# Feed-forward by seven products: adding transfers, splits and loads of the weight sums moved in the order of steps, and one set of token splits moved beside the down products

## The chip, the cores and the metric

The kernel runs on one core of one Trainium2 chip. The metric is the device time of one execution in microseconds (us), here the median of three runs. TensorE (PE) multiplies, VectorE (DVE), ScalarE (ACT) and GpSimd (POOL) do the rest, and SyncE (SP) and POOL issue transfers from memory (HBM) to the on-chip buffers.

## The reference

One inference step of a two-layer trunk (width 1024) over 128 context tokens and 512 latent tokens, 640 in all, with the same weights. Each layer has a first feed-forward, a mixer (a gated DeltaNet, an attention and a recurrent unit side by side), and a second feed-forward. The change touches the feed-forwards alone:

```python
def swiglu(h, w_gu, w_down):
    g, u = jnp.split(h @ w_gu, 2, axis=-1)
    return (jax.nn.silu(g) * u) @ w_down
x = x + 0.5 * mod[:, 2] * swiglu(h, lp['ffn1_wgu'], lp['ffn1_wd'])
```

with `w_gu` of 1024 x 5632 and `w_down` of 2816 x 1024, in f32. The vectors `mod` come from a conditioning vector times `w_mod` (1024 x 9216) for each layer.

## The kernel before, in words

**Split numbers.** An f32 product is made of three faster ones: each operand is split into a high part (ACT rounds a copy, `wh`) and a low part (DVE takes the difference, `wl`), and `three` adds high*high, high*low and low*high. A 128 x 512 piece of weights is thus read by one ACT and one DVE instruction, the split, before PE can use it.

**Seven products.** The 640 tokens are two halves of 320, named p and q, and a column of 128 outputs has a gate part G and an up part U, each with two halves of the 1024 inputs (G1, G2, U1, U2). The four block products of a column are replaced by seven products of sums of tokens with sums of weights (P1, P2, Q3, Q4, Q5, Q6, Q7). Each is 12 matmuls of 320 columns. The sums of tokens are made once for a feed-forward (`sums7`, `split7`). The sums of weights are made by transfers: a tile X is loaded with U2, then U1 is added by a transfer that POOL issues (`more`), and this is the weight of Q5; then G1 is added (the weight of Q6) and then G2 (the weight of Q3). A tile Y is loaded with U1 and gets G1 added (the weight of Q7). P1, P2 and Q4 use G1, G2 and U2 as loaded. A column so takes five loads by SP, four adding transfers by POOL and seven splits. An adding transfer has to wait until the split before it has read the tile.

**Steps.** `ffn7` writes the order of the work by hand. The first columns (chunk 0, 3 or 6 of 22, and 2 more where `then` is 2) go through eight plain products (`eight`), with their down products behind chunk 0. All other columns go by sevens, in chunks of 3 or 4, and each chunk is followed by the 16 down products of 12 matmuls that use it (the last by its own). One product is one step. In the middle of a chunk a column has this order, with its own P1 as step 0: P1, Q4 of the column before, Q5, Q6, P2, Q7, Q3; the next column's P1 is step 7. A column begun before a run of down products has P1 to P2 ahead of it and the rest behind.

`put(t, fn)` hangs other work on a step, and after the matmuls of step t its list is issued, for each engine in this order (`s.pin`, `keep_in_program_order`). Work on steps below 0 and the tail is not pinned: there a scheduler with its own cost model orders the engines, and within a tag buffers are handed out in the order of the program. Among the hung-on work are copies of finished sums out of PSUM by ACT, which the next product into the same bank waits for: t1 after P1 (step 1, before Q6 adds to the bank at step 3), V after Q6 (step 4, before Q7 at step 5). The columns of `mod` for later layers hang on steps too: one transfer of 512 KB and two DVE instructions over 128 x 1024 each (`mod_cols`).

**Buffers.** `w`, raw pieces of weights: 3. `wh` and `wl`: 7 each (`WB`). X: class "B", 4, which the token sums hold until `split7` has read them. Y: two halves of one tile (`rw`).

**Lines.** 157 is `act`, 160 `add`, 164 `more`, 167 `dma`, 170 `tt`, 178 `stt`, 187 `mm`. In the profile t_B is X (and the token sums), t_A on POOL is Y, w a raw piece, tg a copy out of PSUM, th a working tile, t_H the split tokens, t_W and t_C the columns of `mod`; wacc and acc are PSUM banks, wacc that of P1, Q6, Q7 and Q4.

Of the kernel before, what the change touches and what calls it, by code (L numbers as in the profile page):

```python
# [60 lines left out]
K2 = KT // 2  # L61
# [38 lines left out]
class Trunk:  # L100
# [408 lines left out]
    def ffn7(s, wgu, wd, i, spec, done):  # L509
        p, q = HO  # L510
# [8 lines left out]
        def sums():  # L519
            r = [s.A(4 * H, True).v(2, 2, r=True) for _ in range(3 * K2 // 2)]  # L520
            s.s7 = [[r[(3 * k + j) // 2][:, (3 * k + j) % 2] for j in range(3)] for k in range(K2)]

        def rest():
            for k in range(K2):
                v = s.h[k].v(2, r=True)
                s.split(v[:, 0, s.hs(q)], v[:, 1, s.hs(q)], s.xq[k][:, 0])

        acts, w = {}, {0: s.ahead}

        def eight(m0, n, beside):  # L530
            for mi, h in s.halves(n, 2, 0):
                f = m0 + mi
                if f not in w:
                    w[f] = [s.prep(wgu[f, e], KT) for e in range(2)]
                    acts[f] = s.A(2 * T, True)
                g = s.proj(w[f][0], h)
                u = s.proj(w[f][1], h, ps=s.bank())
                s.gated(acts[f], h, g[:, :H], u[:, :H])
                beside()

        acts[0] = s.A(2 * T, True)
        todo = [s.later[:K2], s.later[K2:]] + [[lambda k=k: s.sums7(k)] for k in range(K2)]
        if not then:
            sums()
            todo += [[lambda k=k: s.split7(k)] for k in range(K2)]
        s.first = True

        def beside():
# [18 lines left out]
        if then:  # L567
            sums()
            todo += [[lambda k=k: s.split7(k)] for k in range(K2)]
            eight(n0, then, lambda: [fn() for fn in todo.pop(0)])  # L570
        rest()


        order = []
# [2 lines left out]
        for ci, ch in enumerate(chunks):  # L577
# [19 lines left out]
            else:  # L597
# [3 lines left out]
                a, b = os[:2], os[2:]  # L601
# [6 lines left out]
        def put(t, fn, *a, late=0):  # L608
            at.setdefault(t, ([], [], []))[late].append((fn, a))
# [11 lines left out]
        def tile(f, n, src):  # L621

            def fn():
                ws[f, n] = s.hilo()
                m = len(chunks[f]) if type(n) is int else WK
                wh, wl = ws[f, n]
                s.split(wh[:, :m], wl[:, :m], src()[:, :m])
            return fn

        for f in range(plain, NM):  # L630
            P1, Q5, P2, Q6, Q3, Q7, Q4 = [pos[f, n] for n in ("P1", "Q5", "P2", "Q6", "Q3", "Q7", "Q4")]
            a = P1 - 5
            r, d = {}, {}

            def wsrc(n, f=f):
                return wgu[f, "GU".index(n[0])][:, K2 * (n[1] == "2"):K2 * (n[1] == "2") + K2, :]

            def load(n, src, f=f, r=r, wsrc=wsrc):
                r[n] = rw[:, f % 2] if n == "Y" else s.slots.alloc(WK * P, False, "B").v(WK) if n == "X" else s.raw()
                s.dma(r[n], wsrc(src))  # L640

            def more(n, src, r=r, wsrc=wsrc):
                s.more(r[n], wsrc(src))
            for t, fn, n, src in ((a - 8, load, "X", "U2"), (a - 6, more, "X", "U1"), (a - 3, load, "G1", "G1"),
                                  (a - 2, load, "Y", "U1"), (a + 1, more, "Y", "G1"), (a + 1, load, "G2", "G2"),
                                  (a + 2, more, "X", "G1"), (a + 6, more, "X", "G2"), (max(a + 7, Q4 - 8), load, "U2", "U2")):
                put(t, fn, n, src)


            def tg(n, f=f, d=d):  # L650
                d[n] = s.norm.tile([P, H], F32, name="tg", tag="tg", bufs=3)
                return d[n]

            def th(n, d=d):
                d[n] = s.norm.tile([P, H], F32, name="th", tag="tmp", bufs=4)
                return d[n]
            put(P1 + 1, lambda d=d, tg=tg, f=f: s.act(tg("t1"), prods[f, "b"]))
            put(Q5 + 1, lambda d=d, tg=tg, f=f: s.act(tg("t5"), prods[f, "c"]))
            put(Q6 + 1, lambda d=d, tg=tg, f=f: s.act(tg("V"), prods[f, "b"]))
            put(P2 + 1, lambda d=d, f=f: s.tt(prods[f, "a"], d["t1"], prods[f, "a"], ALU.add))  # L660
            put(Q3 + 1, lambda d=d, f=f: s.tt(prods[f, "c"], d["V"], prods[f, "c"], ALU.add))
            put(Q7 + 1, lambda d=d, f=f: s.tt(d["t5"], d["t5"], prods[f, "b"], ALU.add))

            put(P2 + 2, lambda d=d, th=th, f=f: s.act(th("p"), prods[f, "a"], AF.Tanh, scale=0.5))
            put(P2 + 3, lambda d=d, f=f: s.stt(d["p"], d["p"], 1.0, prods[f, "a"], ALU.add, ALU.mult))
            put(Q3 + 2, lambda d=d, th=th, f=f: s.act(th("q"), prods[f, "c"], AF.Tanh, scale=0.5))
            put(Q3 + 3, lambda d=d, f=f: s.stt(d["q"], d["q"], 1.0, prods[f, "c"], ALU.add, ALU.mult))
            put(Q3 + 3, lambda d=d: s.stt(d["q"], d["q"], -1.0, d["t5"], ALU.mult, ALU.mult))
            put(Q4 + 1, lambda d=d, f=f: s.stt(d["p"], d["p"], -1.0, prods[f, "b"], ALU.mult, ALU.mult))

            def out(f, h):
                if f not in acts:
                    acts[f] = s.A(2 * T, True)
                return acts[f].v(2, r=True)[:, :, s.hs(h)]
            put(Q3 + 4, lambda d=d, f=f: s.act(out(f, q)[:, 0], d["q"]))
            put(Q3 + 4, lambda d=d, f=f: s.tt(out(f, q)[:, 1], d["q"], out(f, q)[:, 0].bitcast(F32), ALU.subtract))
            put(Q4 + 2, lambda d=d, f=f: s.act(out(f, p)[:, 0], d["p"]))
            put(Q4 + 3, lambda d=d, f=f: s.tt(out(f, p)[:, 1], d["p"], out(f, p)[:, 0].bitcast(F32), ALU.subtract))

            for n, x, t in (("P1", "G1", a), ("Q5", "X", a + 1), ("P2", "G2", a + 4), ("Q6", "X", a + 5),  # L680
                            ("Q7", "Y", max(a + 6, Q7 - 5)), ("Q3", "X", max(a + 9, Q3 - 5)), ("Q4", "U2", max(a + 10, Q4 - 5))):
                put(t, tile(f, n, lambda r=r, x=x: r[x]), late=2)
        downs = {}
        for t, x in enumerate(order):
# [12 lines left out]
        n, end = len(s.todo), min(tails) - 8  # L697
        for e, (mc, j, f) in enumerate(s.todo):
            t = e * end // n
# [13 lines left out]
        for t, x in enumerate(order):  # L713
            s.pin = t < min(tails)
            if len(x) == 2:
                f, n = x
# [1047 lines left out]
```

## Time and profile before

| what | value |
|---|---|
| time, median of 3 runs | 3141.28 us (3139.18 to 3144.94) |
| profiled execution: time, span | 3145.61 us, 3143.8 us |
| PE busy, of the span | 3035.8 us, 97% |
| DVE, ACT, POOL busy | 2320.0, 1355.3, 310.2 us |
| granted TensorE clock, mean | 0.989 |

The stretches in which the columns go by sevens, with their down products, are from 208 to 515 us (first feed-forward of layer 0, 14 columns), 1210.5 to 1608 us (second of layer 0, 19 columns), 1778 to 2074 us (first of layer 1, 14 columns) and 2745 us to the end (second of layer 1, 19 columns). The rest of the span is chunk 0, the mixers and the start. A row of instructions gives the start, the duration, the engine, the line and the operation, and in brackets the idle time of the engine before it and what ended it.

### The profile page before, as it was taken

The numbers are of one execution on the slowest core, as the hardware profiler recorded it, in microseconds if no ns is written. First come the engines' busy times: TensorE is split into PE (matmuls) and PEld (weight loads), VectorE is DVE, ScalarE is ACT, GpSimd is POOL, SyncE is SP. The second block draws the span as 40 slices with busy tenths as digits, with TensorE's granted clock in tenths as the row PEclk, the third lists the DMA queues.
The fourth block names the chain that finished last, engine by engine and source line by source line (L and its number), as shares of the span: only waits on it lengthen the run. The fifth ranks groups of instructions, "written<-read, shape, count | busy, mean of one in ns | idle before, by whom it ended". The sixth has DMA issues, their size and how long they took to land. (4 is left out here: it accounts for less than half of the span.)

```text
span 3143.8 us, 54878 instructions
## 1 busy us (share of the span) xinstructions
PE 3035.8 (97%) x20654; PEld 2860.5 (91%) x20654; DVE 2320.0 (74%) x4804; ACT 1355.3 (43%) x2812; POOL 310.2 (10%) x350
## 2 busy tenths in 40 slices
PE   8999999999999999999989999999999999999999
PEld 5999998998887988999989999989989879899999
DVE  6769888767757877777887688786676587866665
ACT  5233335446544443333452333443465454544433
POOL 2011110000000021111120111100000000221111
PEclk9999999999999999999999999999999999999999
DMA  5458773454322416777715577634543224176654
GB/s 223 157 156 224 214 207 107 141 157 125 122 72 62 144 68 173 186 187 189 182 64 167 152 198 196 175 107 130 160 126 100 68 69 145 59 164 152 149 139 127
DMA packets 309000, 451.47 MB, mean 144 GB/s; under 512 B 102989, under 2 KB 147869, under 8 KB 307997
## 3 DMA queue, kind: packets, MB, share of 16 engines
q1 hardware_dynamic: 262076, 357.97, 35.8%
q0 software_dynamic: 38016, 69.22, 13.3%
q10 hardware_dynamic: 8640, 20.76, 1.8%
q8 instruction: 163, 2.67, 0.3%
q14 instruction: 105, 0.85, 0.1%
HBM read 411.87 MB, written 35.96 MB: 142 GB/s over the span
## 5 line engine op out<-in xcount | busy, mean ns | idle before, releaser
L187 PE MATMUL wacc<-t_H,wh 128*128 128x320 f32 x4512 | 1035.0, 314 | 41.7 <-ACT t_H L157 17.3
L187 PEld LDWEIGHTS wacc<-t_H,wh 128*128 128x128 f32 x4512 | 757.8, 188 | 77.2 <-ACT t_H L157 20.7
L187 PE MATMUL acc<-t_A,wh 128*128 128x320 f32 x3440 | 761.5, 308 | 0.3 <-ACT t_A L157 0.3
L187 PE MATMUL wacc<-t_H,wl 128*128 128x320 f32 (+1 forms) x2256 | 702.8, 312 | 3.0 <-DVE wl L170 3.0
L157 ACT ACTIVATE wh<-w 128x512 fp32r<-128x512 f32 (+2 forms) x730 | 439.4, 608 | 572.9 <-PE acc L187 221.3
L170 DVE TENSOR_TENSOR wl<-w,wh 128x512 fp32r<-128x512 f32 (+2 forms) x730 | 483.5, 667 | 170.6 <-ACT wh L157 168.2
L187 PEld LDWEIGHTS acc<-t_A,wh 128*128 128x128 f32 x3440 | 575.5, 188 | 1.1 <-ACT t_A L157 0.5
L187 PE MATMUL acc<-t_A,wl 128*128 128x320 f32 x1720 | 529.8, 308 | 0.2 <-DVE wl L170 0.2
L187 PE MATMUL wacc<-t_A,wh 128*128 128x320 f32 x1984 | 458.6, 313 | 24.9 <-ACT tg L157 19.4
L187 PEld LDWEIGHTS wacc<-t_H,wl 128*128 128x128 f32 (+1 forms) x2256 | 423.8, 188 | 9.8 <-DVE wl L170 4.2
L187 PE MATMUL acc<-t_H,wh 128*128 128x320 f32 x1760 | 400.6, 311 | 0.1
L187 PEld LDWEIGHTS wacc<-t_A,wh 128*128 128x128 f32 x1984 | 336.7, 189 | 35.4 <-ACT tg L157 23.1
L187 PEld LDWEIGHTS acc<-t_A,wl 128*128 128x128 f32 x1720 | 322.6, 188 | 0.4 <-DVE wl L170 0.4
L187 PE MATMUL wacc<-t_A,wl 128*128 128x320 f32 x992 | 309.2, 312 | 0.0
L164 POOL DMA_DIRECT2D t_B<-in_wgu x198 | 194.1, 985 | 1145.4 <-DVE wl L170 682.0
L178 DVE SCALAR_TENSOR_TENSOR t_A<-acc,mG,t_A 128x128 f32<-128x128 f32 (+1 forms) x480 | 201.6, 446 | 138.4 <-PE acc L187 130.6
L187 PEld LDWEIGHTS acc<-t_H,wh 128*128 128x128 f32 x1760 | 299.7, 190 | 1.5 <-ACT wh L157 0.8
L187 PE MATMUL acc<-t_H,wl 128*128 128x320 f32 x880 | 274.7, 313 | 11.2 <-DVE wl L170 11.0
L157 ACT ACTIVATE wh<-t_B 128x512 fp32r<-128x512 f32 x198 | 124.4, 628 | 304.8 <-DMA t_B<-in_wgu 253.0
L170 DVE TENSOR_TENSOR wl<-t_B,wh 128x512 fp32r<-128x512 f32 x198 | 136.2, 688 | 118.5 <-ACT wh L157 118.2
L187 PEld LDWEIGHTS wacc<-t_A,wl 128*128 128x128 f32 x992 | 187.9, 189 | 3.0 <-issue 1.4
L187 PEld LDWEIGHTS acc<-t_H,wl 128*128 128x128 f32 x880 | 166.9, 190 | 16.7 <-DVE wl L170 16.6
(203 smaller groups left out, 3514.7 us busy)
## 6 DMA issues: line engine op xcount, KB each, us to landing
w<-in_wgu SPq DMA_DIRECT2D x286, 256.0 KB, 4.0
t_W<-in_wmod SPq DMA_DIRECT2D x128, 512.0 KB, 4.5
t_B<-in_wgu POOLq DMA_DIRECT2D x198, 256.0 KB, 4.9
w<-in_win SPq DMA_DIRECT2D x168, 256.0 KB, 3.0
w<-in_wd SPq DMA_DIRECT2D x144, 256.0 KB, 3.2
t_B<-in_wgu SPq DMA_DIRECT2D x66, 256.0 KB, 3.9
t_A<-in_wgu SPq DMA_DIRECT2D x66, 256.0 KB, 5.3
t_A<-in_wgu POOLq DMA_DIRECT2D x66, 256.0 KB, 5.2
```

Of the source, the lines that this page charges most:

```text
L157: return s.order(s.nc.scalar.activation(out=out, in_=in_, func=func, **kw))
L164: return s.order(s.nc.gpsimd.dma_start(out=out, in_=in_, accum_op=ALU.add))
L170: return s.order(s.nc.vector.tensor_tensor(out=out, in0=a, in1=b, op=op))
L178: return s.order(s.nc.vector.scalar_tensor_tensor(out=out, in0=a, scalar=sc, in1=b, op0=op0, op1=op1, **kw))
L187: return s.order(s.nc.tensor.matmul(out, lhsT, rhs, start=start, stop=stop, **kw))
```

## The change

It changes the steps on which a column's transfers and splits hang, and the place of `rest`, the splits of the q tokens' sums (four ACT and four DVE instructions over 128 x 320). Steps count from the column's own P1; the value before stands first.

| what | before | after |
|---|---|---|
| load U2 to X; add U1 | -13; -11 | -15; -13 |
| add G1 to X; add G2 to X | -3; 1 | -6; -1 |
| load U1 to Y; add G1 to Y | -7; -4 | -9; -7 |
| load G1; G2; U2 as loaded | -8; -4; 2 | -8; -5; 0 |
| split for P1; Q5; P2; Q6 | -5; -4; -1; 0 | -4; -7; -1; -2 |
| split for Q7; Q3; Q4 | 1; 4; 5 | 1; 3; 4 |

Q7, Q3 and Q4 are split later where down products come between. `rest` is now four pieces, hung on four of the down products of chunk 0 where `then` is 0 (the second feed-forwards); where it is 2 they stay behind the plain products.

```diff
-        def rest():
-            for k in range(K2):
-                v = s.h[k].v(2, r=True)
-                s.split(v[:, 0, s.hs(q)], v[:, 1, s.hs(q)], s.xq[k][:, 0])
+        def rest(k):
+            v = s.h[k].v(2, r=True)
+            s.split(v[:, 0, s.hs(q)], v[:, 1, s.hs(q)], s.xq[k][:, 0])
...
-            todo += [[lambda k=k: s.split7(k)] for k in range(K2)]
+            todo += [[lambda k=k: s.split7(k)] for k in range(K2)] + [[lambda k=k: rest(k)] for k in range(K2)]
...
-        rest()
+            for k in range(K2):
+                rest(k)
...
-            a = P1 - 5
...
-            for t, fn, n, src in ((a - 8, load, "X", "U2"), (a - 6, more, "X", "U1"), (a - 3, load, "G1", "G1"),
-                                  (a - 2, load, "Y", "U1"), (a + 1, more, "Y", "G1"), (a + 1, load, "G2", "G2"),
-                                  (a + 2, more, "X", "G1"), (a + 6, more, "X", "G2"), (max(a + 7, Q4 - 8), load, "U2", "U2")):
+            for t, fn, n, src in ((P1 - 15, load, "X", "U2"), (P1 - 13, more, "X", "U1"), (P1 - 8, load, "G1", "G1"),
+                                  (P1 - 9, load, "Y", "U1"), (P1 - 7, more, "Y", "G1"), (P1 - 5, load, "G2", "G2"),
+                                  (P1 - 6, more, "X", "G1"), (P1 - 1, more, "X", "G2"), (max(P1, Q4 - 9), load, "U2", "U2")):
...
-            for n, x, t in (("P1", "G1", a), ("Q5", "X", a + 1), ("P2", "G2", a + 4), ("Q6", "X", a + 5),
-                            ("Q7", "Y", max(a + 6, Q7 - 5)), ("Q3", "X", max(a + 9, Q3 - 5)), ("Q4", "U2", max(a + 10, Q4 - 5))):
+            for n, x, t in (("Q5", "X", P1 - 7), ("P1", "G1", P1 - 4), ("Q6", "X", P1 - 2), ("P2", "G2", P1 - 1),
+                            ("Q7", "Y", max(P1 + 1, Q7 - 5)), ("Q3", "X", max(P1 + 3, Q3 - 5)), ("Q4", "U2", max(P1 + 4, Q4 - 5))):
```

## Rows read from the trace of the kernel before

**Rows 1.** The page, whole span: busy us, share, instructions of each engine.

```profile
PE 3035.8 (97%) x20654; PEld 2860.5 (91%) x20654; DVE 2320.0 (74%) x4804; ACT 1355.3 (43%) x2812; POOL 310.2 (10%) x350
```

**Rows 2.** Stretches: length, busy us (instructions) of PE, PEld, DVE, ACT, POOL, clock, DMA, GB/s.

```profile
208.00:515.00 307.00, 293.07 (x1948) 288.41 (x1948) 263.31 (x542) 119.55 (x247) 47.17 (x53) 0.99 0.75 202
1210.50:1608.00 397.50, 379.06 (x2514) 371.44 (x2512) 305.38 (x618) 156.12 (x325) 63.83 (x73) 0.99 0.68 177
1778.00:2074.00 296.00, 289.67 (x1951) 287.52 (x1950) 231.23 (x475) 119.81 (x248) 47.28 (x53) 0.99 0.71 182
2745.00:3143.80 398.80, 393.60 (x2678) 392.52 (x2677) 249.29 (x508) 155.54 (x323) 66.44 (x76) 1.00 0.60 146
```

**Rows 3.** Waits of PE, 208 to 515: total us, times, longest us.

```profile
PE wacc L187 <- ACT tg L157: 10.0, 10, 5.0
PE acc L187 <- DVE wl L170: 3.9, 5, 0.9
```

**Rows 4.** Waits of PE, 1210.5 to 1608.

```profile
PE wacc L187 <- ACT tg L157: 12.0, 14, 3.3
PE acc L187 <- DVE wl L170: 4.7, 9, 0.9
PE wacc L187 <- DVE wl L170: 1.7, 1, 1.7
```

**Rows 5.** Waits of PE, 1778 to 2074.

```profile
PE wacc L187 <- ACT tg L157: 3.4, 2, 3.3
PE acc L187 <- DVE wl L170: 1.2, 2, 0.9
```

**Rows 6.** Waits of PE, 2745 to the end.

```profile
PE wacc L187 <- ACT tg L157: 1.4, 2, 0.9
```

**Rows 7.** Stretches from the first Q6 to the first Q7, columns as in rows 2.

```profile
216.92:223.20 6.28, 6.28 (x24) 6.28 (x25) 2.13 (x4) 2.79 (x6) 2.52 (x3) 0.52 0.87 153
1220.34:1226.70 6.36, 6.36 (x24) 6.36 (x25) 2.33 (x4) 2.27 (x5) 3.57 (x4) 0.51 0.52 104
1785.50:1790.60 5.10, 5.10 (x24) 5.10 (x25) 2.13 (x4) 2.79 (x6) 2.53 (x3) 0.67 0.82 127
```

**Rows 8.** Timeline of PE at 1250: a Q6 in the run of columns.

```profile
1250.17 0.56 PE L187 MATMUL wacc<-t_A,wh 128*128 128x320 f32 x2 [1.10 <-ACT tg L157]
```

**Rows 9.** Timeline of ACT: splits for Q6 at 214 and 1249, then t1 and V.

```profile
214.29 0.63 ACT L157 ACTIVATE wh<-t_B 128x512 fp32r<-128x512 f32 x1 [7.10 <-DMA t_B<-in_wgu]
...
1248.84 0.63 ACT L157 ACTIVATE wh<-t_B 128x512 fp32r<-128x512 f32 x1 [5.43 <-DMA t_B<-in_wgu]
...
1249.69 0.43 ACT L157 ACTIVATE tg<-wacc 128x320 f32<-128x320 f32 x1
...
1253.93 0.43 ACT L157 ACTIVATE tg<-wacc 128x320 f32<-128x320 f32 x1
```

**Rows 10.** Timeline of POOL at 1240 and 1250: G1 and G2 added to X.

```profile
1240.15 0.86 POOL L164 DMA_DIRECT2D t_B<-in_wgu  x1 [1.92 <-DVE wl L170]
1250.48 0.86 POOL L164 DMA_DIRECT2D t_B<-in_wgu  x1 [9.47 <-DVE wl L170]
```

**Rows 11.** Waits of ACT, 1231 to 1608, the longest in total.

```profile
ACT wh L157 <- DMA t_B<-in_wgu: 78.9, 18, 8.2
```

**Rows 12.** Tile t_B, 1231 to 1608: its transfers.

```profile
DMA to landing us min/median/max: 3.6/4.9/9.2
```

**Rows 13.** Stretches of one column each, columns as in rows 2.

```profile
372.97:388.80 15.83, 13.12 (x87) 12.33 (x85) 12.65 (x25) 6.37 (x14) 3.51 (x4) 1.00 0.86 220
...
1258.54:1273.57 15.03, 13.12 (x86) 12.34 (x85) 10.46 (x21) 6.37 (x14) 2.62 (x3) 1.00 0.74 170
2841.00:2853.40 12.40, 12.40 (x87) 12.40 (x86) 7.91 (x18) 1.98 (x4) 1.83 (x3) 1.00 0.63 166
```

**Rows 14.** Stretch up to the first Q6 of layer 0's second feed-forward, columns as before.

```profile
1196.50:1217.00 20.50, 18.58 (x124) 17.82 (x122) 20.14 (x45) 2.31 (x4) 1.73 (x2) 1.00 0.52 170
```

**Rows 15.** Groups of DVE, 1189 to 1212: the low parts of the moved token splits.

```profile
L170 DVE TENSOR_TENSOR t_H<-t_A,t_H 128x320 fp32r<-128x320 f32 x4 | 1.8, 482 | 0.0
```

## The prediction

> **What bounds the kernel now.** I read the page first: PE is busy 97% of the span [rows 1], so a change pays only where PE stands still or runs at its lower clock. Then the stretches: by busy against length, PE is idle 13.9 us in the first feed-forward of layer 0 (call it A), 18.4 in the second (B), 6.3 in the first of layer 1 (C) and 5.2 in the last (D) [rows 2]. Then the waits of PE in each: nearly all idle time is one product waiting either for a copy out of PSUM by ACT ("tg", 10.0, 12.0, 3.4 and 1.4 us in A, B, C, D) or for the low part of a split by DVE ("wl", 3.9 in A, 4.7 and 1.7 in B, 1.2 in C) [rows 3 to 6]. That is 13.9 + 18.4 + 4.6 + 1.4 = 38.3 us.
>
> The longest of these waits, 5.0, 3.3 and 3.3, stand at the first Q6 of A, B and C, and behind each PE runs on a granted clock of 0.52, 0.51 and 0.67, its lower level of 1.2 GHz for all or part of it: two products of 24 matmuls take 6.28, 6.36 and 5.10 us [rows 7]. A column of seven products without a wait takes 12.40 us [rows 13], a step 12.40/7 = 1.77, two steps 3.54. The lower clock so costs 2.7 + 2.8 + 1.6 = 7.1 us. **All that could come back is 38.3 + 7.1 = 45.4 us:** 7.7 (5.0 + 2.7) at the start of A, 7.8 (3.3 + 1.7 + 2.8) of B, 4.9 (3.3 + 1.6) of C, and in the run of columns 8.9 in A, 13.4 in B, 1.3 in C, 1.4 in D.
>
> Why a copy is late is read from three timelines. POOL issues the transfer that adds G1 to X at 1240.15, after a wait for the low part of Q5's split [rows 10]. ACT stands from 5.43 us before 1248.84 at the split for Q6, waiting for it; t1, the copy that Q6 needs, is behind it at 1249.69 [rows 9], and Q6 starts at 1250.17, 1.10 late [rows 8]. So the transfer took 8.7 us to land, and ACT's order turns this into a wait of PE. In B the split waits so 18 times, 78.9 us in all, up to 8.2 [rows 11]; ACT's idle time costs only what reaches t1, or V, which a late ACT and DVE then bring late too, and the low part for Q3 behind them.
>
> **The adding of G1 and the split for Q6.** From the add's step to Q6 are 6 steps before (-3 to 3), 10.6 us, and 9 after (-6 to 3), 15.9. The example needs 8.7 for landing and 1.3 (1248.84 to 1250.17) from split to product, 10.0, and came too late because the add itself waited for DVE. The longest wait in the runs cannot be more than the 3.3 of B's start, and 5.3 us of new lead covers it. Adding G2 and the split for Q3 gain one step between them (3 to 4), 1.77 us, and the low part for Q3 is hung one step sooner; the longest "wl" waits are 0.9 [rows 3, 4]. So these waits should go where DVE and the transfers have time to spare.
>
> They have in B, C and D: DVE is busy 305 of 397.5, 231 of 296 and 249 of 398.8 [rows 2]. In A it is not so plain. A column beside which two columns of modulation are made takes DVE 12.65 us and the transfer engines 0.86 x 15.83 = 13.6 us, against PE's 12.40; with one pair DVE takes 10.46 [rows 13]. Between such columns stand others and the down products, with less for both (A as a whole: 263 of 307, and 0.75) [rows 2], so lag is made and paid back, but some of A's waits will stay. I take half of A's 8.9, 4.5; of B's 13.4, 10.5 (a few columns with two pairs, and the one behind the start); 0.9 of C's 1.3 and 1.2 of D's 1.4. **Sum in the runs: 17.1.** The ends: 25.0 if all goes, and a loss, by the mechanism of the second rival.
>
> The Trainium skill, DMA: Bandwidth & Descriptors, section Anatomy of one DMA, fits a transfer from GpSimd as 2.0 us plus its bytes by 436,000 per us; by that 256 KB would land in 2.6 us, three steps of lead would have been ample, and the runs would give back nothing: with the 9 of the starts alone, 3132. The trace disagrees: the landings are 3.6 us at least, 4.9 in the median and 9.2 at most [rows 12].
>
> **The starts.** There the chain begins when `split7` sets a buffer of class B free, which the change does not move, and POOL's adds come one behind another. So the landing itself comes little sooner. But in A the split for Q6 starts at 214.29 [rows 9] and Q6 at 216.92 [rows 7]: 2.6 us, of which the split is 0.63 and 2.0 is t1 standing in ACT's pinned order behind it and behind what DVE owes. After the change that split hangs at -2, below step 0, where t1 need not stand behind it. I take this 2.0 off in A and C. Against it stands a new wait: V now comes behind the split for Q3 and that for the next P1. G2's add is issued when Q6's split is done, about when Q6 starts; 3.6 to land at least [rows 12], 0.63 and 0.63 for the two splits, 0.43 for V [rows 9] make 5.3 against the 3.54 of Q6 and P2: 1.8 us late, or none where the lower clock stretches the two products to 6.3. So A: 5.0 - 2.0 + 1.8 = 4.8 for 7.7, a gain of 3; C: 3.3 - 2.0 + 1.8 = 3.1 for 4.9, a gain of 2.
>
> In B DVE is full before the first products, 20.14 of 20.50 us [rows 14], and the wait of 1.7 there is P1's for its low part [rows 4]. Three or four of the moved token splits stand in this stretch, 0.48 each [rows 15]; hung on earlier down products they leave it 1.4 shorter. Q5's split is now ahead of P1's, which brings the add of G1 forward by about as much. I put P1's wait at 0.3, Q6's at 1.7, V's at 1.8, 3.8 for 7.8: a gain of 4. D has no wait at its start and loses none. **Sum of the starts: 9.** The ends: all 20.4; or 5.4 lost, three times 1.8, if nothing is sooner and the clock stays up.
>
> **What else moves.** SP's five loads and POOL's four adds per column stay as many, so do seven splits on ACT and seven on DVE. SP's X, Y and U2 are 2 steps sooner, but SP waits only for buffers. A raw piece is held 4 steps for 3: 12 of 21 buffer-steps a column. The split pairs are held 9 + 4 + 5 + 5 + 4 + 3 + 4 = 34 steps in all for 28, of 49, and in the last down products of a chunk all 7 pairs are held at once: two down, Q7, Q3 and Q4 of one column, Q5 and P1 of the next. I count this at nothing, since the eighth comes only after a down product has given one back. If one were missing, a split would wait for a down product of 1.77 at most, at 14 ends of chunks: 25 us. The moved token splits cost nothing more than they did, beside down products that keep PE busy 18.58 of 20.50 [rows 14]; without that cover they would hold `x_update` by 0.48 each, 2 us in a feed-forward. The new wait of t1 for the split of the next column's Q5, hung at step 0, is for an add issued 6 steps (10.6 us) before, longer than the longest landing of 9.2 [rows 12].
>
> **Sum:** 17.1 + 9 = 26 us off the profiled execution's 3145.6, so 3119.5; the median of the runs is 4.3 below that execution, so **3115**.
>
> **Rivals.** (1) Layer 0 stays bound by DVE and transfers: its runs give nothing, the rest 9 + 2.1 = 11, so 3130. For it the column at 373, both over PE's 12.40; against it B, where DVE has 92 us to spare [rows 2, 13]. Chance 0.21. The skill's fit above would lead to nearly the same time, 3132.
>
> (2) Slower: the split for Q3 now stands ahead of V, and V must end before step 5. From the add of G2 (-1) there are 6 steps, 10.6 us, less 0.63 + 0.63 + 0.43: 8.9 for POOL's wait and the landing. Past that every Q7 waits. If DVE lags 3 us with Q6's low part, a landing of 5.9 suffices, and the median is 4.9 [rows 12]. At 1 us for each of the 66 columns, 66 - 26: 3181; it decides from 0.4 us a column. Against it: G2's add is the first after POOL has been idle, 9.47 us in the example [rows 10], and V at 1253.93 [rows 9] was itself delayed by what goes. Chance 0.07.
>
> (3) Everything comes back, the clock at the starts too: 45, so 3096. For it the lead of 5.3 us against the 1.10 of the example [rows 8]; against it the starts, whose landing hardly moves. Chance 0.12.
>
> (4) No change: earlier loads and adds only make each other slower, landings grow by what the lead grows, and the same buffers set the pace; 3141. For it the transfers' share of 0.86 [rows 13]; against it C and D, which run nearly without waits at 0.71 and 0.60 [rows 2]. Chance 0.07.
>
> **The numbers.** My forecast, 3105 to 3127, has 0.53. About 0.2% (6.3 us) is what a measurement of this kernel can tell from no change; the forecast, (1) and (3) are faster by more: 0.86. (4) is the same, 0.07, and (2) slower, 0.07. The range goes from most of (3) to past (1): 3099 to 3135, with some of (3) and all of (2) and (4) outside.
>
> **What would show it.** In B the waits of PE for "tg" fall from 12.0 to some 5 or less, with the rest at the start, and ACT's wait for X (78.9) falls to a third. In A DVE's share rises and "wl" or "tg" waits stay. At the starts the split for Q6 no longer stands ahead of t1, and the first Q7 waits for V. It is wrong if new waits for "tg" stand at Q7 in the run of C or D, if a split waits for PE at the ends of chunks, or if POOL's adds wait for DVE as long as now and the landing of X still ends ACT's longest waits.

## The result, and the profile after

Time after: **3106.56 us** (median of 4 runs, 3104.22 to 3112.2); before, on the same chip, 3142.14 (3139.18 to 3144.94). The ratio is 0.9893, 95% interval 0.9881 to 0.9906: 35.6 us, 1.1%, faster. The profiled execution took 3105.24 us for 3145.61. The forecast was 3115, 3099 to 3135. So sign and size came out; of its two large terms one was half of what was measured and the other four times too large, and the reason given for the first was not the whole mechanism.

The page's first part after, to set against [rows 1]: PE is busy 15 us less with the same 20654 matmuls, and DVE, ACT and POOL run the same instructions as before, ACT 14 us longer in all.

```profile
PE 3020.4 (97%) x20654; PEld 2860.3 (92%) x20654; DVE 2322.1 (75%) x4804; ACT 1369.3 (44%) x2812; POOL 310.1 (10%) x350
```

To see where, both traces are cut at the same matmuls (there the order on PE did not change, but for seven matmuls at D's start; in the mixers between them some changed places): the start of a feed-forward runs from shortly ahead of its first P1 (in B 100 matmuls) to its first Q7, the run from there to the end of the stage. Columns as in [rows 2]. First two runs of before (A, B), whose answers in the second fence are lines two and four:

```profile
223.27:511.06 287.79, 278.83 (x1875) 274.83 (x1874) 256.65 (x529) 113.69 (x235) 43.66 (x49) 1.00 0.76 206
1226.74:1604.10 377.36, 364.15 (x2442) 357.87 (x2440) 293.07 (x593) 150.86 (x314) 59.40 (x68) 1.00 0.69 181
```

After: start and run of A, start and run of B, start of C.

```profile
207.55:222.72 15.17, 9.95 (x53) 9.69 (x51) 5.19 (x9) 5.66 (x12) 2.62 (x3) 0.77 0.81 194
222.72:498.31 275.59, 274.98 (x1876) 274.72 (x1875) 256.35 (x528) 114.27 (x234) 43.68 (x49) 1.00 0.78 215
1180.09:1205.84 25.75, 23.66 (x152) 23.39 (x150) 21.36 (x44) 6.11 (x12) 5.26 (x6) 0.93 0.64 171
1205.84:1565.88 360.04, 358.90 (x2441) 357.73 (x2440) 293.81 (x593) 155.70 (x314) 59.40 (x68) 1.00 0.73 190
1737.66:1754.88 17.22, 12.47 (x67) 12.21 (x66) 6.69 (x13) 7.14 (x16) 3.53 (x5) 0.80 0.86 188
```

The runs gave back 12.2 (A), 17.3 (B), 2.6 (C) and 1.7 us (D), 33.8 in all; the starts 0.1 (A, 15.29 before) and 4.9 (B, 30.67), while C's lost 2.6 (14.61). That is 36.2 of the profiled 40.4; 4.2 came elsewhere, where nothing was edited. In the profiled executions of all kernels below, the time outside these stretches, from the first matmul to the last, lay between 1720.7 and 1733.4, so 4 us there mean nothing.

The waits of PE after, in A, in B (three lines), in C and in D, to set against [rows 3 to 6] (total, times, longest):

```profile
PE wacc L187 <- ACT tg L157: 5.8, 2, 5.2
...
PE wacc L187 <- DVE wl L170: 2.1, 1, 2.1
PE wacc L187 <- ACT tg L157: 0.9, 2, 0.6
PE acc L187 <- DVE wl L170: 0.2, 1, 0.2
...
PE wacc L187 <- ACT tg L157: 4.7, 1, 4.7
...
PE wacc L187 <- DVE t_A L178: 0.2, 1, 0.2
```

What is left are the three starts (5.2 at the first Q6 of A, 4.7 of C, 2.1 at the first P1 of B) and 1.9 us in 66 columns.

### The profile page after: what moved, and what is told of

Same layout as the page of the kernel before. It is cut to its first block, busy times and chain, and to the rows that moved or that the text cites. A ratio compares the mean times of both kernels' runs of the same rounds, so it can differ in the third digit from the quotient of the medians.

```text
span 3103.4 us, 54871 instructions
## 1 busy us (share of the span) xinstructions
PE 3020.4 (97%) x20654; PEld 2860.3 (92%) x20654; DVE 2322.1 (75%) x4804; ACT 1369.3 (44%) x2812; POOL 310.1 (10%) x350
## 5 line engine op out<-in xcount | busy, mean ns | idle before, releaser
L187 PEld LDWEIGHTS wacc<-t_A,wh 128*128 128x128 f32 x1984 | 338.2, 190 | 22.6 <-ACT tg L157 11.7
L164 POOL DMA_DIRECT2D t_B<-in_wgu x198 | 173.2, 946 | 1140.8 <-DVE wl L170 614.2
L157 ACT ACTIVATE tg<-wacc 128x320 f32<-128x320 f32 x236 | 102.0, 433 | 169.1 <-PE wacc L187 143.1
```

Source lines behind the costliest of these rows:

```text
L157: return s.order(s.nc.scalar.activation(out=out, in_=in_, func=func, **kw))
L164: return s.order(s.nc.gpsimd.dma_start(out=out, in_=in_, accum_op=ALU.add))
L187: return s.order(s.nc.tensor.matmul(out, lhsT, rhs, start=start, stop=stop, **kw))
```

## The experiments

Each is given with its ratio to the kernel before, run on the same chip, and with what the same matmuls took, in us. The diffs show only the entries that change.

| kernel | ratio, 95% interval | A start, run | B start, run | C start, run | D run |
|---|---|---|---|---|---|
| before | 1 | 15.3, 287.8 | 30.7, 377.4 | 14.6, 286.9 | 382.6 |
| after | 0.9893 (0.9881 to 0.9906) | 15.2, 275.6 | 25.7, 360.0 | 17.2, 284.3 | 380.9 |
| E1 rest alone | 1.0001 (0.9989 to 1.0012) | 15.1, 288.0 | 27.5, 377.6 | 15.4, 290.5 | 381.0 |
| E2 steps alone | 0.9898 (0.9882 to 0.9915) | 14.9, 275.7 | 28.1, 359.0 | 17.9, 284.3 | 382.8 |
| E3 add of G1 three steps sooner | 0.9893 (0.9876 to 0.9910) | 15.2, 275.6 | 28.0, 363.2 | 17.1, 284.9 | 380.5 |
| E4 all but X | 1.0020 (1.0010 to 1.0030) | 16.5, 286.1 | 33.6, 371.8 | 17.5, 290.8 | 381.5 |
| E5 one step sooner | 0.9968 (0.9956 to 0.9979) | 13.8, 286.7 | 30.9, 369.7 | 15.5, 286.9 | 380.5 |
| E6 first in POOL's queue | 1.0009 (1.0000 to 1.0018) | 15.1, 291.6 | 29.1, 377.1 | 14.7, 290.5 | 380.9 |
| E7 and Q5's split sooner | 0.9901 (0.9884 to 0.9917) | 15.8, 276.9 | 25.2, 362.1 | 15.7, 284.9 | 380.5 |
| E8 t1 ahead of the splits | 0.9895 (0.9881 to 0.9909) | 10.7, 279.8 | 25.7, 361.0 | 14.1, 285.4 | 382.4 |
| E9 Y's add behind X's | 0.9870 (0.9854 to 0.9885) | 12.9, 276.1 | 24.8, 361.4 | 15.3, 284.3 | 381.7 |
| E10 both | 0.9880 (0.9868 to 0.9893) | 8.2, 279.8 | 25.0, 363.6 | 11.1, 287.7 | 382.5 |
| E11 start ordered | 0.9895 (0.9881 to 0.9908) | 7.8, 282.5 | 24.6, 365.0 | 10.2, 288.3 | 382.4 |
| E12 and `mod` later | 0.9906 (0.9892 to 0.9920) | 8.2, 282.8 | 24.4, 366.2 | 11.4, 289.1 | 384.1 |

### Which part of the change

**E1**, `rest` alone: the hunks on `rest` in the kernel before, nothing else.

> The kernel before with one part of the change: the q tokens' splits (rest) hung on down products of chunk 0 in the second feed-forwards; all steps of transfers and splits as before. In the changed kernel the waits at the start of B fell from 1.7 + 3.3 us with a slow clock behind them (2.8) to 2.1 + 0 with a shorter slow stretch, while the starts of A and C, where rest stays where it was, kept a wait of 5.2 and 4.7. Theory: the moved splits are what freed the start of B, so this kernel takes 3.5 to 5 us off: 3137 to 3139. Rival: the earlier steps freed it, and rest alone gives nothing or under 1.5 us: 3141 to 3142.

3144.35 us, no change. B's start is 3.1 shorter, which the interval cannot tell from nothing; Q6's wait of 3.3 stayed, P1's 1.7 went.

**E2**, the changed kernel without the hunks on `rest`.

> The changed kernel with rest put back behind the plain products; all moved steps stay. Theory: the gain in the runs of columns (about 34 us between the two profiled executions, the same matmuls compared) is all here, and only the start of B loses, by 3.5 to 5: 3110 to 3112. Rival (the steps freed the start of B too): 3106 to 3107.5. If the two moves only work together, B's start is as late as before in this kernel and in the one with rest alone.

3111.58. B's start is 2.5 shorter than before: here Q6's wait went and P1's is 3.3. So each of the two took one wait of B's start, where I had expected the moved splits to take both, and the steps alone make P1's longer; together they take 4.9. The gain in the runs is all here.

**E3**, the add of G1 three steps sooner, the other steps as before:

```diff
-(a - 8, load, "X", "U2"), (a - 6, more, "X", "U1"), (a + 2, more, "X", "G1")
+(a - 10, load, "X", "U2"), (a - 8, more, "X", "U1"), (a - 1, more, "X", "G1")
-("Q5", "X", a + 1)
+("Q5", "X", a - 2)
```

> The kernel before with only the chain up to the adding of G1 to X begun sooner: U2's load to -15, U1's add to -13, the split for Q5 to -7, G1's add to -6 (nine steps ahead of Q6 for six); the split for Q6 stays at 0, G2's add at 1, everything else as before. Theory: the waits of the runs come from this one landing, so at least three quarters of the runs' 34 us come back: 3108 to 3116. Rival: the earlier splits (Q6 from 0 to -2, Q3, Q4) and the earlier G2 are needed as well, and this kernel gives under half: 3125 or more.

3110.71: the whole gain, with four of the thirteen moved steps. The split for Q6 on its old step, G2, Y, Q3, Q4 and the raw pieces were not needed.

**E4**, the moved steps that do not touch X:

```diff
-(a - 2, load, "Y", "U1"), (a + 1, more, "Y", "G1"), (a + 1, load, "G2", "G2")
+(a - 4, load, "Y", "U1"), (a - 2, more, "Y", "G1"), (a, load, "G2", "G2")
-(max(a + 7, Q4 - 8), load, "U2", "U2")
+(max(a + 5, Q4 - 9), load, "U2", "U2")
-("P1", "G1", a)
+("P1", "G1", a + 1)
-("Q4", "U2", max(a + 10, Q4 - 5))
+("Q4", "U2", max(a + 9, Q4 - 5))
```

> The kernel before with the moved steps that do not touch X: Y's load and add to -9 and -7, G2's load to -5, U2's to 0, the split for P1 to -4 and for Q4 to 4. Theory: these carry no wait of PE, so no change within 0.2%: 3139 to 3145; or some us slower, because Y's add then stands one step ahead of G1's add to X, which is still at -3, and the transfers share the same engines. Rival: Q4's and P1's splits and the raw pieces are part of the gain: 3130 or less.

3148.2, slower by 0.2%, as the second half of the theory had it: with Y's add ahead of X's the first Q6 waits 7.4, 6.6 and 6.0 us in A, B and C. In the runs of B it gave 5.6 back.

### Is it the lead, the place in the queue, or something else

**E5**, the chain of E3 begun one step sooner instead of three.

> The kernel before with the chain up to G1's add to X begun one step sooner instead of three (U2 at -14, U1 at -12, split for Q5 at -5, G1's add at -4): seven steps ahead of Q6 for six. Theory (the waits of the runs are the tail of one landing, up to 1.2 us in the columns): one step of 1.77 covers most of them, 60 to 90 per cent of what three steps gave (33): 3114 to 3124. Rival (the landing stretches as far as the lead, or the whole chain's lag adds up from column to column): under 40 per cent, 3130 or more.

3134.52. My theory failed: one step of 1.77, longer than the longest wait in the runs (1.4), brought a third of the gain. In B ACT still waits for X (81.2 us in 25 waits). In its trace (start, duration, engine, line, operation, idle time before) POOL issues the add of G1 at 1243.34, ACT stands at the split for Q6 until 1251.39, and the next add of G1 is issued at 1256.74:

```profile
1243.34 0.86 POOL L164 DMA_DIRECT2D t_B<-in_wgu  x1 [1.05 <-DVE wl L170]
1253.05 1.75 POOL L164 DMA_DIRECT2D t_B<-in_wgu  x2 [8.85 <-DVE wl L170]
1254.12 1.57 POOL L164 DMA_DIRECT2D t_A<-in_wgu  x1
1256.74 0.86 POOL L164 DMA_DIRECT2D t_B<-in_wgu  x1 [1.05 <-DVE wl L170]
...
1251.39 0.63 ACT L157 ACTIVATE wh<-t_B 128x512 fp32r<-128x512 f32 x1 [4.40 <-DMA t_B<-in_wgu]
...
1253.61 0.63 ACT L157 ACTIVATE wh<-t_B 128x512 fp32r<-128x512 f32 x1
```

The add was issued sooner, and landed after 7.6 us in the median over B's columns, for 6.4 before: three adds issued in one burst, at 1239.64 to 1240.71, stood ahead of it. So was it the place in the queue?

**E6**: G1's add on its old step, but ahead of the two others of that burst.

```diff
-(a - 6, more, "X", "U1"), (a + 1, more, "Y", "G1"), (a + 2, more, "X", "G1")
+(a - 5, more, "X", "U1"), (a + 2, more, "X", "G1"), (a + 2, more, "Y", "G1")
```

> The kernel before with G1's add to X on its old step (-3, six steps ahead of Q6), but first in POOL's queue: the add of U1 to the next column's X moves from -11 to -10 and Y's add from -4 to -3, both then issued behind it on the same step. In the kernel before G1's add is issued behind three others and lands after 6.4 us in the median in B (17 columns), 8.7 at most; in the kernel with one step more of lead it still stood behind them, took 7.6, and gave a third of the gain; with three steps more it was issued ahead of the next U1 and took 5.2. Queue theory (adding transfers are served one after another, and the place in the queue decides): G1's landing falls to 5 or less and half or more of the 33 come back without any lead: 3112 to 3127. Lead theory: no change or a loss, 3140 to 3148.

3147.42. The queue theory alone fell too: the landing did fall, to 5.2 in the median, and the time did not.

**The loop.** What E5 and E6 share with before: the add of G1 to column f's X must wait until DVE has read X for Q5's low part; the split for Q5 of column f stands on ACT behind the split for Q6 of column f-1; and that one waits for the landing of G1's add of column f-1. This closes a loop from column to column: landing, plus ACT's and DVE's work from the one split to the other. In E5 above it is 8.05 (1243.34 to 1251.39) and 5.35 (to 1256.74), 13.4, and PE needs 12.4 for a column: each column then comes later than the one before, until down products come between. Read from the traces, as means over the 12 columns of B that have the next column right behind them (no down products between, the first two columns left out), with what B's run took above that of the changed kernel:

| kernel | landing | wait to the split | split to the next add | add to add | B's run |
|---|---|---|---|---|---|
| before | 7.2 | 0.1 | 6.7 | 14.0 | +17.3 |
| E5 | 7.8 | 0.1 | 5.7 | 13.6 | +9.6 |
| E6 | 6.1 | 0.1 | 7.7 | 13.9 | +17.1 |
| E3 | 4.7 | 2.2 | 5.4 | 12.3 | +3.1 |
| after | 5.9 | 0.3 | 6.0 | 12.1 | 0 |

The first three lie 1.2 to 1.6 above PE's pace, 15 to 20 us over these columns. E6 shows why the queue alone gave nothing: the 1.1 that the landing won, ACT's and DVE's part lost again (1.0). In E3 the loop keeps PE's pace with 2.2 to spare. In D before, counted in the same way, it took 6.1 + 0.1 + 6.7 = 12.9 (the 11.7 in the expectation of E7 adds medians that take in columns ahead of down products, and is too low). That is 0.5 above the pace, and D hardly waited: over the three or four columns of a chunk so little stays within the lead.

**E7** takes the loop apart without the lead: E6, and the split for Q5 two steps sooner; G1's add keeps its old step.

```diff
-(a - 8, load, "X", "U2"), (a - 5, more, "X", "U1")
+(a - 9, load, "X", "U2"), (a - 7, more, "X", "U1")
-("Q5", "X", a + 1)
+("Q5", "X", a - 1)
```

> The kernel with G1's add first in the queue on its old step (-3), and beyond that the split for Q5 two steps sooner (-6 for -4, with the add of U1 at -12 and the load of U2 at -14, for its sake). G1's add to X keeps its step, six ahead of Q6. Loop theory: what repeats from column to column is landing of G1's add + ACT's and DVE's work from the split for Q6 to the low part for the next column's Q5, for which the next add of G1 waits; in B the medians were 6.4 + 0.1 + 6.8 = 13.3 us in the kernel before, 7.6 + 0.1 + 5.4 = 13.1 with the lead of seven, 5.2 + 0.1 + 7.5 = 12.8 with the queue's order, all above the 12.4 that PE needs for a column, and in D before 5.4 + 0.1 + 6.2 = 11.7, below it, without waits. Here the second part falls by 2 to 3.5, the sum under 12.4, and the waits of the runs go though the add hangs where it did: 3110 to 3122. Theory of the step's lead (the add's step against Q6's is what counts): as the kernel before, 3140 to 3148.

3111.75: nearly the whole gain with the add on its old step. The same means in B are 5.6 + 0.3 + 6.4, from add to add 12.35: PE sets the pace. Here, as in E3, G1's add also stands further ahead among the adds than before; by E6 that alone gives nothing, but the earlier split for Q5 in the old order was not run. In its trace the add at 1224.40 has just landed (1229.84) when ACT comes to the split for Q6 at 1229.92 (no wait), and before the next column's split for Q5 (1234.66) ACT now stands for PE (0.85) and DVE, not for a transfer; the next add is at 1236.39, 12.0 us after the first. The last line is B's run, columns as in [rows 2].

```profile
1224.40 0.86 POOL L164 DMA_DIRECT2D t_B<-in_wgu  x1 [1.40 <-DVE wl L170]
...
1236.39 0.86 POOL L164 DMA_DIRECT2D t_B<-in_wgu  x1 [0.86 <-DVE wl L170]
...
1229.92 0.63 ACT L157 ACTIVATE wh<-t_B 128x512 fp32r<-128x512 f32 x1
1232.52 0.44 ACT L157 ACTIVATE th<-acc 128x320 f32<-128x320 f32 x1 [1.97 <-DVE acc L170]
1233.81 0.44 ACT L157 ACTIVATE tg<-wacc 128x320 f32<-128x320 f32 x1 [0.85 <-PE wacc L187]
1234.14 0.62 ACT L157 ACTIVATE wh<-t_A 128x512 fp32r<-128x512 f32 x1
1234.66 0.62 ACT L157 ACTIVATE wh<-t_B 128x512 fp32r<-128x512 f32 x1
...
1211.62:1573.67 362.05, 360.04 (x2441) 359.26 (x2440) 293.76 (x593) 154.68 (x314) 60.10 (x69) 1.00 0.74 190
```

### The starts

**E8**, the changed kernel, t1 ahead of the splits (e is the column's number in the run, from 0):

```diff
-(P1 - 6, more, "X", "G1"), (P1 - 1, more, "X", "G2")
+(2 if e == 1 else P1 - 6, more, "X", "G1"), (P1 + 2 if e == 0 else P1 - 1, more, "X", "G2")
-("Q5", "X", P1 - 7), ("Q6", "X", P1 - 2), ("P2", "G2", P1 - 1)
+("Q5", "X", 1 if e == 1 else P1 - 7), ("Q6", "X", P1 + 1 if e == 0 else P1 - 2), ("P2", "G2", P1 + 1 if e == 0 else P1 - 1)
```

> The changed kernel, but for the first two columns by sevens of each feed-forward ACT's copy t1 stands ahead of the splits: the first column's splits for Q6 and P2 hang at step 1 behind t1 (G2's add to X at 2), the second column's split for Q5 at step 1 of the first (its G1 add at 2). In the changed kernel G1's add lands at 213.03 in A and 1744.85 in C, and Q6 starts at 216.75 and 1748.57, 3.7 us later, of which the split, its low part and the first matmul's start need 1.4. Theory (the order of ACT costs the starts): Q6 2.2 us sooner in A and in C, 4 to 6 in all with less of the lower clock: 3101 to 3103. Rival (the landing and DVE's queue set Q6): within 2 of the changed kernel, 3105 to 3109.

3112.39, no gain. ACT's order did cost the starts 4.5 (A) and 3.2 (C), but the runs behind lost 4.2, 1.0, 1.1 and 1.5: the later adds make Q3, and the second column, late.

**E9**, Y's add at -5 for the first two columns, in the order of the program (pinned; the lines that pin it are not shown):

```diff
-(P1 - 7, more, "Y", "G1")
+(P1 - 5 if e < 2 else P1 - 7, more, "Y", "G1")
```

> The changed kernel, but for the first two columns by sevens the adds of G1 to Y stand on POOL behind the add of G1 to X (at step -5, in the order of the program). In the changed kernel the add to Y was issued 0.54 us ahead of the one to X in both starts and landed 3.1 us ahead of it in A (209.96, 213.03) and 1.4 in C. In the kernel with Y's add moved sooner and X's not, Q6's waits at the starts were 7.4, 6.6 and 6.1 for 5.0, 3.3 and 3.3. Theory (the transfer ahead in POOL's queue delays the one that Q6 needs): X lands 3 us sooner in A and 1.4 to 4 in C, and Q6 follows: 3099 to 3103. Rival (all transfers share the bandwidth and the order matters little): 3105 to 3109.

3104.08. The first Q6 waits 3.7 and 3.9 for 5.2 and 4.7, the starts are 2.3 and 2.0 shorter and little is given back. Its ratio is the best of all, but its interval reaches into that of the changed kernel.

**E10**, E8 and E9 together.

> Both edits of the starts at once: Y's adds behind X's, and t1 ahead of the splits. If both theories hold, A's and C's first Q6 wait under 2 us each and the products behind them run at the full clock: 3092 to 3099. If only one of the two counts, as that one alone.

3105.62: A's and C's starts 6.9 and 6.1 shorter, the runs 12.7 longer in all (4.2, 3.5, 3.3, 1.6).

**E11**, the second column's adds behind G1's of the first (the lines that pin them are not shown):

```diff
-(P1 - 13, more, "X", "U1"), (P1 - 7, more, "Y", "G1"), (P1 - 6, more, "X", "G1")
+(-5 if e == 1 else P1 - 13, more, "X", "U1"), (P1 - 5 if e < 2 else P1 - 7, more, "Y", "G1"), (4 if e == 1 else P1 - 6, more, "X", "G1")
-("Q5", "X", P1 - 7)
+("Q5", "X", 3 if e == 1 else P1 - 7)
```

> The changed kernel with the start of each feed-forward ordered for the queue: G1's add to the first column's X ahead of all of the second column's adds and of Y's (U1 to the second X and Y's add at -5, pinned in this order), the second column's split for Q5 at step 3 behind V, its G1 add at 4. Queue theory: G1 lands 4 to 5 us sooner in A and C, so Q6 waits under 2 us for 5.2 and 4.8 and the products behind run at the full clock; 8 to 13 us off, some 3 given back where the second column's adds now come later: 3095 to 3102. Rival (what the first column gains the second one loses in the same queue): 3103 to 3108.

3113.66, above even the range of the rival (the kernel before took 3146.23 on this chip), but by the rival's mechanism. A's start runs without a wait at the full clock, 7.77 us for 15.17, and its run loses 6.9. The lines: A's start and run, its longest wait of PE, and ACT at 223.77 and DVE behind it. It is now Q4's, at 225.67, for a sum that DVE makes at 225.04, behind the low part for the second column's Q6, for whose G1 ACT had waited 5.67.

```profile
209.15:216.92 7.77, 7.60 (x53) 7.34 (x52) 4.38 (x8) 5.04 (x11) 2.64 (x3) 1.00 1.04 225
216.92:499.41 282.49, 277.98 (x1876) 277.42 (x1874) 258.13 (x530) 115.38 (x237) 44.53 (x50) 0.99 0.78 213
...
PE wacc L187 <- DVE tg L170: 3.3, 1, 3.3
...
223.77 0.63 ACT L157 ACTIVATE wh<-t_B 128x512 fp32r<-128x512 f32 x1 [5.67 <-DMA t_B<-in_wgu]
...
224.43 0.69 DVE L170 TENSOR_TENSOR wl<-t_B,wh 128x512 fp32r<-128x512 f32 x1 [3.91 <-ACT wh L157]
225.04 0.48 DVE L170 TENSOR_TENSOR tg<-tg,wacc 128x320 f32<-128x320 f32 x1
```

**E12**, E11 with the columns of `mod` kept off the starts: those on steps begin at step 6, none on the last four down products of chunk 0.

> The kernel with the start ordered for the queue, and the columns of modulation kept off the starts: those on steps begin 6 steps later and are packed into the rest, and none hangs on the last four down products of chunk 0, where DVE was 98% busy before B's first product. Theory: B's wait of P1 (2.1) goes and A's and C's start have 512 KB less on the transfer engines: 3 to 6 us below the kernel without this. Rival (A's columns are full: denser modulation brings back waits of PE there, as the first rival of the forecast had it): same as or above that kernel, with waits in A's run.

3115.25, no gain. P1's wait in B fell from 2.1 to 0.9, and the wait at the second column was 3.7 in A, 4.8 in B. At the starts POOL issues the first columns' adds one behind another; in E8, E10 and E11 what was put first made something else late.

## Why the prediction was right, point by point

**The runs: right that they carry the gain, and its size half of what it was.** Forecast 17.1, at most 25.0; measured 33.8, above the upper end. Two things were mis-sized.

*The price of a wait.* I counted only PE's idle time. In B's run the idle time fell from 13.2 (377.36 - 364.15) to 1.1, but PE's busy time for the same matmuls also fell, by 5.2; in A's by 3.9. There were 21 and 14 waits of over 0.1 us, 3 and 1 after: about 0.3 each. A wait in the trace of before shows why:

```profile
225.03 0.45 PE L187 MATMUL acc<-t_H,wh 128*128 128x320 f32 x2
225.76 0.42 PE L187 MATMUL acc<-t_H,wl 128*128 128x320 f32 x1 [0.28 <-DVE wl L170]
226.02 0.31 PE L187 MATMUL acc<-t_H,wh 128*128 128x320 f32 x1
```

Matmuls follow at 0.15 (12.40 us for 84); the second of the first row began at 225.18, so the next came 0.58 later, and the one behind it 0.26 later. That is 0.54 lost, where the row says 0.28: 0.15 is the tail of the last matmul, which nothing overlaps and which counts as busy, and 0.11 the slower matmul behind the wait. [Rows 13] had it: 87 matmuls with waits took 13.12 us of busy time, without 12.40, and I subtracted only the waits.

*A's half.* I let half of A's waits stay because DVE was busy 12.65 in a column with two columns of `mod`, against PE's 12.40. But those 12.65 stood in a stretch stretched by waits to 15.83 us, and it held other work of DVE too. The same matmuls after, with two columns of `mod` again:

```profile
368.95:381.27 12.32, 12.32 (x87) 12.32 (x86) 11.93 (x24) 7.06 (x15) 2.94 (x4) 1.00 1.03 280
```

DVE has 11.93 beside them: less than PE, and one split less than in the longer stretch. The busy time of a stretch with waits must be set against the stretch's length. The first rival, layer 0 bound by DVE and transfers, fell with it.

**The reason: part of it.** The example of late copies was read right: add, landing, split, t1, Q6. "It came too late because the add itself waited for DVE" was the place to go on asking what DVE waited for. I took the lead in steps, 5.3 us more against 1.1 missing, as the cure; by that E5 would have done with 1.77, and E7 could not have worked. What the moved steps did was to shorten the loop: between the split for Q6 and the next column's for Q5 lie two steps for three. In B it now takes 5.9 + 0.3 + 6.0 = 12.1 in the means: just under PE's 12.4, without the 2.2 to spare of E3. What still comes late stays short of t1, since the split for Q6 is two steps sooner; how much each of the two does in the changed kernel was not separated. ACT's wait for X in B, 78.9 in [rows 11], is 24.5 in 15 waits, the third that was forecast, with landings no shorter than in [rows 12] (B's run, and the transfers of t_B):

```profile
ACT wh L157 <- DMA t_B<-in_wgu: 24.5, 15, 5.1
...
DMA to landing us min/median/max: 3.6/5.3/9.0
```

The fourth rival, transfers that only make each other slower, had this much in it: landings in B grew from 4.9 to 5.3 in the median, and in E5 G1's own from 6.4 to 7.6.

**The starts: wrong.** Forecast 3 + 4 + 2 = 9; measured 0.1, 4.9 and -2.6. The step that failed is "After the change that split hangs at -2, below step 0, where t1 need not stand behind it". A split on an earlier step stands further ahead in ACT's order, so t1 stays behind it, and now behind the splits for P2 and the next Q5 too:

```profile
213.11 0.63 ACT L157 ACTIVATE wh<-t_B 128x512 fp32r<-128x512 f32 x1 [6.80 <-DMA t_B<-in_wgu]
213.65 0.45 ACT L157 ACTIVATE t_H<-t_A 128x320 fp32r<-128x320 f32 x1
214.01 0.61 ACT L157 ACTIVATE wh<-w 128x512 fp32r<-128x512 f32 x1
214.53 0.61 ACT L157 ACTIVATE wh<-t_B 128x512 fp32r<-128x512 f32 x1
215.90 0.47 ACT L157 ACTIVATE t_A<-th 128x320 fp32r<-128x320 f32 x1 [0.76 <-DVE th L170]
216.27 0.42 ACT L157 ACTIVATE tg<-wacc 128x320 f32<-128x320 f32 x1
```

Q6 starts at 216.75, 3.6 behind the split, for 2.6 before. From the first matmul of the stretch the split starts 0.75 sooner (213.11 - 207.55 for 214.29 - 207.98), and this is lost again. E8 shows that the order was worth 4.5 and 3.2 there, and that it is paid back. The clock behind the first Q6, to set against [rows 7] for A, B and C (lines one, three and four), and behind the first P1 of B (line two):

```profile
216.75:222.72 5.97, 5.97 (x25) 5.97 (x25) 2.22 (x4) 2.78 (x6) 1.75 (x2) 0.56 0.96 250
1197.45:1202.32 4.87, 4.87 (x23) 4.87 (x23) 2.92 (x5) 2.49 (x5) 0.84 (x1) 0.65 0.77 209
1202.32:1205.84 3.52, 3.52 (x27) 3.52 (x25) 1.44 (x3) 1.42 (x4) 1.79 (x3) 1.00 0.84 187
1748.57:1754.88 6.31, 6.31 (x24) 6.31 (x25) 2.23 (x4) 3.31 (x7) 1.75 (x2) 0.53 1.05 239
```

C's wait grew from 3.3 to 4.7, and the granted clock behind it fell from 0.67 to 0.53, 1.2 GHz for nearly all of the two products. In B, Q6's wait and the slow clock behind it are gone, but a slow stretch now stands behind P1's wait of 2.1: 4.87 us at 0.65 for 23 matmuls that take 3.4 at 0.15. Before, PE ran at 0.15 a matmul there, behind a wait of 1.7. The forecast had no term for this.

**The new wait of V never came**, nor did the second rival: no PE wait stands at a first Q7, and in the runs V is at most 0.6 late. In the first column no Q4 stands between P1 and Q5, so V hangs on step 3, the same as the split for Q3, and is issued ahead of it; I had counted with the middle of a chunk. **B's start** was forecast at a gain of 4 and gave 4.9, but not as written: P1's wait is 2.1, not 0.3, and Q6's and V's are 0. **Buffers, loads, the seven held pairs** cost nothing that shows, as forecast: the longest wait of a split for PE in the runs is 4.7, before 5.7, and C and D show no new wait in theirs.

So 16.7 us too little in the runs, 6.7 too much at the starts and 4.2 from elsewhere make the 14.3 by which the profiled execution (3105.2) stands below the sum (3119.5); on the median the forecast was 8.4 off. That the total lies inside the range is in part luck: with the starts at the 9 that were forecast, these runs alone would have given 3145.6 - 33.8 - 9 - 4.3 = 3098.5, just below it.

## What to carry to other kernels

When a copy is late column after column, follow the chain back until it meets itself: if it closes over an engine's order, add up the loop and compare it with the pace of the engine that should be the bound. Where the loop was 1.6 above that pace, one step of lead brought a third of the gain (E5), and a shorter loop nearly all of it with the late add on its old step (E7). Price a short wait of PE at its idle time plus the 0.3 us measured here, and compare a busy time only with the length of its own stretch.

## What was not expected of the hardware

Adding transfers issued by POOL in one burst landed one behind another: in B before, four issued at 1250.48, 1251.02, 1251.56 and 1255.05 landed at 1254.08, 1256.48, 1259.94 and 1263.78, 2.4 to 3.8 us apart. How many are ahead is a part of a landing, and not all of it: G1's add took 6.4 in the median as the fourth of them and 5.2 as the second (E3), but also 5.2 as the first of its burst (E6).
